# MLP second product: the fifth sub-product beside the sixth, the seventh and the fourth alone, and one weight combination made by transfers

## Chip, cores and metric

One core of a Trainium2 chip runs the whole program. The metric is device time in microseconds (us), the median of repeated executions; times in the profile come from one further execution that the hardware profiler recorded. Engines are named as in the profile: PE (matrix multiply), PEld (its weight loads), DVE (vector), ACT (activation), POOL, SP. SP, ACT and POOL also issue transfers (DMA).

## The reference

One layer of a diffusion backbone, fp32. Only its last third matters here, the MLP with its normalised and gated residual:

```python
def _sq_relu_mlp(h, w1, w2):
    return jnp.square(jax.nn.relu(h @ w1)) @ w2
...
        y_x = _sq_relu_mlp(_modulate(x, g_pre_mlp[l], sh2, sc2), w_mlp_in[l], w_mlp_out[l])
        x = x + gt2 * _rmsnorm(y_x, g_post_mlp[l])
```

`x` is 1024 tokens by 1024, the hidden layer 4096 wide. The second product, hidden (1024x4096) by `w2` (4096x1024), is the subject.

## The kernel before

**Products.** Each fp32 matmul is made of three on numbers split into a high part (`..h`, rounded, by ACT, line 169) and a low part (`..l`, the rest, by DVE, line 175): high·high, low·high, high·low (`three`, lines 221 to 223). The second product is one level of a seven-product scheme (Strassen-Winograd). With A the 2x2 blocks of the hidden layer (rows: token halves; columns: interleaved halves of the 4096) and B those of `w2`, it needs

- P1 = A11·B11, P2 = A12·B21, P4 = A22·T4, P5 = S1·T1, P6 = S2·T2, P7 = S3·T3, and a third one, S4·B22, which is itself made of seven smaller products (`INNER`, M1 to M7);
- of the weights T1 = B12−B11, T2 = B22−T1, T3 = B22−B12, T4 = T2−B21 (one sign is kept the other way round in the code);
- results: C11 = P1+P2; u2 = P1+P6; u4 = u2+P5; C12 = u4 + third; C22 = u4+P7; C21 = u2+P7 with P4.

C11 and C12 are the two halves of the output of tokens 0 to 511 (rows 0 to 3, 128 tokens each), C21 and C22 those of tokens 512 to 1023 (rows 4 to 7).

**Stages.** A product runs over 8 groups g of the 4096 (`NG`), and in each over four token tiles t: 24 matmuls of 128x512 (`group`). Its sums stand in four PSUM banks: `pyx` (P1, P2), `pyy` (P6), `pyv` (P7, then P4 on top of it), `pyz` (P5). The order of the groups is the list `items`; at the start of each group `prepare()` makes the operands of an item three places ahead: load the hidden block (`hr..`), load and combine weights, split both. The profile leaves out the first digit of a name: `t_4h` is `t1_4h` to `t4_4h`; `hrS`, `hhS` are of S1, S2, S3, `hrA`, `hhA` of A11, A12, A22; `b` are blocks of `w2`.

Before the change the order is P6 with P7 by turns (8 groups each), then P4 groups 0 to 3 by turns with P5 groups 0 to 3, then P5 groups 4 to 7, then P4 groups 4 to 7, the last two stretches token tile by token tile at the end, so that a tile can be finished when its sums end. In P6, DVE makes T1, T3 and T2 from loads of B12 and B22 (lines 2053 to 2056); for P4 it loads B22 and B21 again and makes T4 from them (lines 2063, 2064).

**Finishing a row.** `gated`: ACT squares and sums a half row (line 154), DVE multiplies it by the gate (line 2200); `finish` also asks for the inverse root of both halves' sums (DVE line 161, POOL line 163, `ry`); `end` multiplies the row by it, adds the residual (`xo`, loaded from `x1d`; DVE line 2208) and sends it out (line 2209). Row 7 is done in quarters at the very end (`pyw` is a second bank for its second quarter; lines 2217, 2348, 2352, 2354, 2357).

**Order and buffers.** In this part PE, ACT, DVE and SP keep the order in which the code is written; POOL keeps its own program order. Loads of weights use 4 buffers (`wraw`), hidden loads 4 (`tmp` "h"), weight splits 4 pairs (`whl`), all else a pool of 33 pages (`page`). An instruction that needs a buffer waits until its last user is done.

Of the kernel before, what the change touches and what calls it, by code (L numbers as in the profile page):

```python
# [18 lines left out]
P = 128  # L19
# [3 lines left out]
NT = SEQ // P  # L23
# [80 lines left out]
def hybrid_block(ctx, tc, x, ctx_in, w_mod, mod_pages, w_u, b_mod, gp1, gp2, w_in, pool_w, rpb, w_out, w1, w2, vectors,  # L104
# [1414 lines left out]
    with tc.tile_pool(name="ps2", bufs=6, space=PSUM) as ps2:  # L1519
# [7 lines left out]
      with ExitStack() as tmp2:  # L1527
# [487 lines left out]


        w2v = w2.rearrange("(k i p) n -> i p k n", i=2, p=P)
        t1, t3 = {}, {}
# [5 lines left out]
        def wcols(name, i, h, g):  # L2024
            return columns(wraw.tile([P, 1024], F32, tag="raw", name=f"{name}_{g}"), i, h, g)
# [15 lines left out]
        def operands(name, g, made=None):  # L2041
            made = made or high_low
            if name == "P1":
                t1[g] = columns(page(f"b11_{g}"), 0, 0, g)
                return hidden("A11", g, g <= AHEAD + 1), made(f"b11_{g}", t1[g])
            if name == "P2":
                return hidden("A12", g), made(f"b21_{g}", wcols("b21", 1, 0, g))
            if name in INNER:
                return inner_operands(name, g)
            if name == "P6":  # L2050

                b12, b22 = wcols("b12", 0, 1, g), wcols("b22", 1, 1, g)
# [10 lines left out]
            nc.vector.tensor_tensor(b22, b22, t1[g], sub)  # L2063
            nc.vector.tensor_tensor(b21, b21, b22, sub)
# [96 lines left out]
        with tc.issue_after(first[ET.PE]), in_order(ET.PE, ET.Activation, ET.DVE, ET.SP):  # L2161
# [5 lines left out]
            def four(name):  # L2167
                return [bank(f"{name}_{t}") for t in range(4)]
# [37 lines left out]
            def end():  # L2206
                for m, rs, xt in ending:
                    nc.vector.scalar_tensor_tensor(xt, rows[m], rs, xt, mul, add)  # L2208
# [83 lines left out]
            for t in range(4):  # L2292
                rows[t] = page(f"row{t}")
                gated(t, 0, x[t])
            y, v = four("pyy"), four("pyv")
            for g in range(NG):
                group(y, "P6", g)
                if g == NG - 1:
                    u2 = halves("u2")
                    for t in range(4):  # L2300
                        nc.vector.tensor_tensor(u2[t], y[t], s1[t], add)
                group(v, "P7", g)
            for t in range(4):
                rows[4 + t] = page(f"row{4 + t}")
                nc.vector.tensor_tensor(half(4 + t, 1), v[t], u2[t], add)
            z = four("pyz")
            u4 = [inner_part(f"c{t // 2}")[:, t % 2 * 512 : t % 2 * 512 + 512] for t in range(4)]
            for g in range(NG // 2):
                group(v, "P4", g, more=True, last=(g == NG // 2 - 1))
                group(z, "P5", g)  # L2310
                nc.vector.tensor_tensor(u4[g], u4[g], u2[g], add)
            for g in range(NG // 2, NG - 2):
                group(z, "P5", g)
            while coming:
                prepare()

            for t in range(4):
                cs = slice(0, 512 if t < 3 else 256)
                nc.vector.tensor_tensor(v[t][:, cs], v[t][:, cs], u2[t][:, cs], add)
            xts = {}  # L2320
            for m in range(4):
                xts[m] = wraw.tile([P, 1024], F32, tag="raw", name=f"xo{m}")
            for m in range(4, NT):
                xts[m] = page(f"xo{m}")
            for m in range(NT):
                nc.sync.dma_start(xts[m], x1d[m])
# [64 lines left out]
```

## Time and profile before

| | us |
|---|---|
| median of 3 runs | 1027.67 (1027.49 to 1028.32) |
| the profiled execution, its own time | 1027.31 |
| its span, first to last instruction | 1025.5 |
| what lies around the span | 1.8 |
| PE busy | 1006.3 (98% of the span) |
| DVE busy | 795.2 (78%) |
| ACT busy | 559.4 (55%) |
| POOL busy | 154.6 (15%) |

"Busy" of PE is modelled, since matmuls overlap. A timeline row reads: start, duration, engine, line, operation, output<-inputs, shape, and in brackets the engine's idle time before it with what released it. In the part in question, P6 starts at 836.6 us and the last matmul at 1014.0 us.

### The profile page before, as it was taken

What the parts mean: (1) busy time and instruction counts of PE and PEld (TensorE: products, weight loads), DVE (VectorE), ACT (ScalarE), POOL (GpSimd) and SP (SyncE); (2) the same over time, 40 slices, a digit from 0 to 9 for tenths busy, and PEclk for the clock granted to TensorE, in tenths of its full rate; (3) what the DMA queues carried; (4) which work ended last, traced back from release to release, by engine and by line L of the source; (5) the groups of instructions that cost most, each with busy time, mean ns of one, the idle gap of its engine ahead of it and who ended that gap; (6) DMA issues with size and microseconds to landing.
All of it is one profiled execution on the core that took longest, in us unless ns stands there. A gap on an engine that the chain in (4) does not pass through costs nothing. (4 is left out here: it accounts for less than half of the span.)

```text
span 1025.5 us, 16659 instructions
## 1 busy us (share of the span) xinstructions
PE 1006.3 (98%) x6154; PEld 838.3 (82%) x6154; DVE 795.2 (78%) x1217; ACT 559.4 (55%) x974; POOL 154.6 (15%) x234
## 2 busy tenths in 40 slices
PE   8999999999999999999999999999999999999995
PEld 5788888878998888888888888888888888887874
DVE  5588757977885788879988888656787898768587
ACT  6672354348886747786554554546564444334333
POOL 4111200266773221400000000000000000000001
PEclk9999999999999999999999999999999999999998
DMA  9899898541447946886876567348976766554374
GB/s 363 316 294 302 262 262 286 205 103 43 104 98 204 235 169 200 278 216 208 265 255 216 184 210 257 123 159 268 335 267 213 263 246 229 197 194 173 114 285 166
DMA packets 126594, 224.85 MB, mean 219 GB/s; under 512 B 9584, under 2 KB 61680, under 8 KB 126512
## 3 DMA queue, kind: packets, MB, share of 16 engines
q1 hardware_dynamic: 100016, 173.24, 49.9%
q0 software_dynamic: 9360, 19.58, 9.3%
q10 hardware_dynamic: 17136, 30.97, 8.1%
q8 instruction: 48, 0.79, 0.3%
q14 instruction: 34, 0.28, 0.1%
HBM read 170.25 MB, written 52.45 MB: 217 GB/s over the span
## 5 line engine op out<-in xcount | busy, mean ns | idle before, releaser
L1234 ACT ACTIVATE sp<-sp,nm 128x640 f32<-128x640 f32 (+1 forms) x64 | 51.3, 802 | 10.9 <-DVE ri L1238 5.1
L1223 DVE CUSTOM_DVE_ANT_0 sp<-S,tab 128x640 f32<-128x640 f32 (+1 forms) x56 | 44.5, 795 | 14.0 <-PE pz L1254 9.1
L1857 ACT ACTIVATE c<-c 128x512 f32<-128x512 f32 x48 | 30.3, 632 | 44.3 <-DVE c L1979 25.0
L169 ACT CAST wpS<-S 128x512 fp32r<-128x512 f32 x64 | 38.7, 616 | 28.0 <-PE phv L223 10.1
L221 PE MATMUL phx<-thB,wpA 128*128 128x512 f32 x128 | 50.2, 392 | 0.0
L223 PE MATMUL phx<-thB,wpA 128*128 128x512 f32 x128 | 49.8, 389 | 0.0
L222 PE MATMUL phx<-tlB,wpA 128*128 128x512 f32 x128 | 49.8, 389 | 0.0
L175 DVE TENSOR_TENSOR wpS<-S,wpS 128x512 fp32r<-128x512 f32 x64 | 43.4, 686 | 7.5 <-ACT wpS L169 7.5
L163 POOL TENSOR_TENSOR ry<-vy,nhalf 128x1 f32<-128x1 f32 x7 | 5.4, 767 | 285.0 <-DVE vy L161 285.0
L1858 ACT ACTIVATE c<-c 128x512 f32<-128x512 f32 x48 | 30.3, 631 | 15.1 <-DVE sa L1942 12.1
L221 PEld LDWEIGHTS phx<-thB,wpA 128*128 128x128 f32 x128 | 24.0, 188 | 5.5 <-ACT s L1910 0.4
L223 PEld LDWEIGHTS phx<-thB,wpA 128*128 128x128 f32 x128 | 24.0, 188 | 5.1
L222 PEld LDWEIGHTS phx<-tlB,wpA 128*128 128x128 f32 x128 | 24.0, 188 | 4.9
L1273 DVE COPY pt<-T 128x512 f32<-128x512 f32 x32 | 21.9, 686 | 5.6 <-PE T L1254 5.6
L1288 PE MATMUL pa<-pt,v 128*64 128x128 f32 x352 | 25.9, 279 | 0.2
L221 PE MATMUL phz<-thB,wpS 128*128 128x512 f32 x64 | 25.0, 391 | 0.0
L221 PE MATMUL phv<-thT,wpA 128*128 128x512 f32 x64 | 25.0, 391 | 0.0
L223 PE MATMUL phv<-thT,wpA 128*128 128x512 f32 x64 | 24.9, 389 | 0.0
L223 PE MATMUL phz<-thB,wpS 128*128 128x512 f32 x64 | 24.9, 389 | 0.0
L222 PE MATMUL phz<-tlB,wpS 128*128 128x512 f32 x64 | 24.9, 389 | 0.0
L222 PE MATMUL phv<-tlT,wpA 128*128 128x512 f32 x64 | 24.9, 389 | 0.0
L221 PE MATMUL phy<-thT,wpS 128*128 128x512 f32 x64 | 24.9, 389 | 0.0
(1178 smaller groups left out, 3553.6 us busy)
## 6 DMA issues: line engine op xcount, KB each, us to landing
b<-in_w SPq DMA_DIRECT2D x48, 512.0 KB, 4.3
hrA<-hdA SPq DMA_DIRECT2D x24, 512.0 KB, 5.5
hrS<-hdS SPq DMA_DIRECT2D x24, 512.0 KB, 5.3
wm<-in_mod_pages SPq DMA_DIRECT2D x16, 512.0 KB, 9.4
wa_0w<-in_w SPq DMA_DIRECT2D x16, 512.0 KB, 5.0
wa_1w<-in_w SPq DMA_DIRECT2D x16, 512.0 KB, 4.3
hdA<-c ACTq DMA_DIRECT2D x32, 256.0 KB, 2.2
hdS<-sa ACTq DMA_DIRECT2D x32, 256.0 KB, 2.2
```

The costliest lines, as they stand in the source:

```text
L163: nc.gpsimd.tensor_tensor(r, v, nhalf, ALU.pow)
L169: nc.scalar.copy(hi, src)
L175: nc.vector.tensor_tensor(lo, src, hi.bitcast(F32), sub)
L221: nc.tensor.matmul(ps, ahi, bhi, start=first, stop=False, skip_group_check=more)
L222: nc.tensor.matmul(ps, ahi, blo, start=False, stop=False, skip_group_check=more)
L223: nc.tensor.matmul(ps, alo, bhi, start=False, stop=last, skip_group_check=more)
L1223: nc.vector.tensor_tensor_reduce(out=to, in0=s, in1=bt, scale=1.0, scalar=BIG, op0=add, op1=ALU.min, accum_out=nm)
L1234: nc.scalar.activation(sp, sp, AF.Exp, bias=least[i, e], scale=-1.0, accum_out=sums[i][:, e : e + 1])
L1273: copy(turns[i].rearrange("p e i t -> p (e i) t")[:, :, h * HD : (h + 1) * HD], turned[i][h].rearrange("p (a t) -> p a t", a=8))
L1288: nc.tensor.matmul(pa[e * HD : (e + 1) * HD, cols], v[:, f : f + HD], turns[i][:, e, c] if c < 4 else fifths[i][:, :, (e + 1) * HD : (e + ...
L1857: nc.scalar.activation(r, src, AF.Relu)
L1858: nc.scalar.activation(r, r, AF.Square)
```

## The change

P5 takes the place of P7 beside P6; then come the 8 groups of P7, then the 8 of P4, of which the last four are done token tile by token tile as before.

- T3 is still made beside T1 and T2, but P7 comes later now: POOL stores it to DRAM (`t3d`), and SP loads it again for P7 (8 stores, 8 loads of 512 KB).
- T2 goes to a page of its own, with its sign turned (its split turns it back, line 177 instead of 175). After the split, a transfer issued by POOL adds B21 from DRAM to that page (`last_added`, `add_to`), which makes T4: 8 adding transfers of 512 KB. The second loads of B22 and B21 (16 of 512 KB) and DVE's lines 2063 and 2064 (8 each) go.
- u4 is made from `pyz` and u2 when P5 is complete, C12 from it; rows 0 to 3 are finished while P7 runs, one per group from the second on, and sent out by POOL. The residuals of rows 0 to 3 are loaded in P7's first four groups, those of rows 4 to 7 at the end.
- C22 is made after P7; its squares and gate products stand in P4's first four groups.

```diff
-                nc.vector.tensor_tensor(b12, b22, b12, sub)
-                t3[g] = b12
-                nc.vector.tensor_tensor(b22, b22, t1[g], sub)
-                return hidden("S2", g), made(f"t2_{g}", b22)
+                t2[g] = page(f"t2_{g}")
+                nc.vector.tensor_tensor(t2[g], t1[g], b22, sub)
+                nc.vector.tensor_tensor(b12, b22, b12, sub)
+                nc.gpsimd.dma_start(t3d[g], b12)
+                parts = hidden("S2", g), high_low(f"t2_{g}", t2[g], -1.0)
+                if g < NG - 2:
+                    last_added(g)
+                return parts
...
             if name == "P7":
-                return hidden("S3", g), made(f"t3_{g}", t3.pop(g))
-            b22, b21 = wcols("b22", 1, 1, g), wcols("b21", 1, 0, g)
-            nc.vector.tensor_tensor(b22, b22, t1[g], sub)
-            nc.vector.tensor_tensor(b21, b21, b22, sub)
-            return hidden("A22", g), made(f"t4_{g}", b21)
+                r = wraw.tile([P, 1024], F32, tag="raw", name=f"t3_{g}")
+                nc.sync.dma_start(r, t3d[g])
+                if g in (2, 3):
+                    last_added(NG - 4 + g)
+                return hidden("S3", g), made(f"t3_{g}", r)
+            return hidden("A22", g), made(f"t4_{g}", t2.pop(g))
+        t3d = [dram.tile([P, 1024], F32, tag=f"t3_{g}", name=f"t3_{g}") for g in range(NG)]
+        def last_added(g):
+            add_to(t2[g].rearrange("p (a f) -> p a f", a=2), w2v[1][:, 2 * g : 2 * g + 2, :512])
...
-        items += [(n, g) for g in range(NG) for n in ("P6", "P7")]
-        items += [(n, g) for g in range(NG // 2) for n in ("P4", "P5")] + [("P5", g) for g in range(NG // 2, NG)]
-        items += [("P4", g) for g in range(NG // 2, NG)]
+        items += [(n, g) for g in range(NG) for n in ("P6", "P5")]
+        items += [(n, g) for n in ("P7", "P4") for g in range(NG)]
...
-                    nc.sync.dma_start(og[m], xt)
+                    (nc.gpsimd if m < 4 else nc.sync).dma_start(og[m], xt)
...
-            y, v = four("pyy"), four("pyv")
+            y, z = four("pyy"), four("pyz")
...
+                group(z, "P5", g)
+            def residual(m):
+                xts[m] = page(f"xo{m}")
+                nc.sync.dma_start(xts[m], x1d[m])
+            v, u4 = four("pyv"), halves("u4")
+            for g in range(NG):
                 group(v, "P7", g)
+                if g < 4:
+                    residual(g)
+                    nc.vector.tensor_tensor(u4[g], z[g], u2[g], add)
+                    nc.vector.tensor_tensor(c12[g], c12[g], u4[g], add)
+                if 0 < g < 5:
+                    finish(g - 1, 1, c12[g - 1], xts[g - 1])
+            end()
             for t in range(4):
                 rows[4 + t] = page(f"row{4 + t}")
-                nc.vector.tensor_tensor(half(4 + t, 1), v[t], u2[t], add)
+                nc.vector.tensor_tensor(half(4 + t, 1), v[t], u4[t], add)
             for g in range(NG // 2):
                 group(v, "P4", g, more=True, last=(g == NG // 2 - 1))
-                group(z, "P5", g)
-                nc.vector.tensor_tensor(u4[g], u4[g], u2[g], add)
-            for g in range(NG // 2, NG - 2):
-                group(z, "P5", g)
-            while coming:
-                prepare()
+                gated(4 + g, 1, half(4 + g, 1))
+            side = bank("pyw")[:, :256]
             for t in range(4):
                 cs = slice(0, 512 if t < 3 else 256)
                 nc.vector.tensor_tensor(v[t][:, cs], v[t][:, cs], u2[t][:, cs], add)
-            for t in range(4):
-                token_sums(z, t, [made["P5", g] for g in (NG - 2, NG - 1)], False, True, False)
-                c = half(4 + t, 1)
-                nc.vector.tensor_tensor(c, c, z[t], add)
-                gated(4 + t, 1, c)
-                finish(t, 1, z[t], xts[t], u4[t])
-                if t == 1:
-                    side = bank("pyw")[:, :256]
-                    nc.vector.tensor_tensor(side, v[3][:, 256:], u2[3][:, 256:], add)
+            nc.vector.tensor_tensor(side, v[3][:, 256:], u2[3][:, 256:], add)
+            while coming:
+                prepare()
+            for m in range(4, NT):
+                residual(m)
```

Three places in the order of instructions, before and after. First DVE where P7 ends and P4's first group is to go on top of its sums; `u2` is u2, `row4` to `row7` take C22. Before:

```order
L2301 TENSOR_TENSOR u21_9816<-pyy_3_9252,s11_8547 128x512
L2063 TENSOR_TENSOR b22_1_9821<-b22_1_9821,b11_1_8043 128x1024
L2064 TENSOR_TENSOR b21_1_9823<-b21_1_9823,b22_1_9821 128x1024
L175 TENSOR_TENSOR hhA22_1l_9830<-hrA22_1_9827,hhA22_1h_9829 128x1024
L175 TENSOR_TENSOR t4_1l_9834<-b21_1_9823,t4_1h_9833 128x1024
L2305 TENSOR_TENSOR row4_9861<-pyv_0_9253,u20_9815 128x512
L2305 TENSOR_TENSOR row5_9863<-pyv_1_9254,u20_9815 128x512
```

After:

```order
L175 TENSOR_TENSOR hhA22_2l_10194<-hrA22_2_10191,hhA22_2h_10193 128x1024
L175 TENSOR_TENSOR t4_2l_10198<-t2_2_9310,t4_2h_10197 128x1024
L2217 SCALAR_TENSOR_TENSOR xo3_10065<-row3_9259,ry_3_10120,xo3_10065 128x1024
L2332 TENSOR_TENSOR row4_10227<-pyv_0_9886,u40_9890 128x512
L2332 TENSOR_TENSOR row5_10229<-pyv_1_9887,u40_9890 128x512
```

The sum for u2 and the two steps that make a T4 no longer stand ahead of the copies of P7's sums; the last step of row 3 does.

Second, DVE where P4's last four groups begin (`pyv` gets u2 added there) and what follows. Before:

```order
L2063 TENSOR_TENSOR b22_7_10267<-b22_7_10267,b11_7_8400 128x1024
L2064 TENSOR_TENSOR b21_7_10269<-b21_7_10269,b22_7_10267 128x1024
L175 TENSOR_TENSOR hhA22_7l_10276<-hrA22_7_10273,hhA22_7h_10275 128x1024
L175 TENSOR_TENSOR t4_7l_10280<-b21_7_10269,t4_7h_10279 128x1024
L2319 TENSOR_TENSOR pyv_0_9253<-pyv_0_9253,u20_9815 128x512
L2319 TENSOR_TENSOR pyv_1_9254<-pyv_1_9254,u20_9815 128x512
L2319 TENSOR_TENSOR pyv_2_9255<-pyv_2_9255,u21_9816 128x512
L2319 TENSOR_TENSOR pyv_3_9256<-pyv_3_9256,u21_9816 128x256
L2330 TENSOR_TENSOR row4_9861<-row4_9861,pyz_0_9869 128x512
L2200 TENSOR_TENSOR row4_9861<-row4_9861,Gb_8997 128x512
L2222 TENSOR_TENSOR c0_10319<-pyz_0_9869,c0i_8916 128x512
```

After:

```order
L2339 TENSOR_TENSOR pyv_0_9886<-pyv_0_9886,u20_9843 128x512
L2339 TENSOR_TENSOR pyv_1_9887<-pyv_1_9887,u20_9843 128x512
L2339 TENSOR_TENSOR pyv_2_9888<-pyv_2_9888,u21_9844 128x512
L2339 TENSOR_TENSOR pyv_3_9889<-pyv_3_9889,u21_9844 128x256
L2340 TENSOR_TENSOR pyw_10383<-pyv_3_9889,u21_9844 128x256
L175 TENSOR_TENSOR hhA22_7l_10392<-hrA22_7_10389,hhA22_7h_10391 128x1024
L175 TENSOR_TENSOR t4_7l_10396<-t2_7_9699,t4_7h_10395 128x1024
L161 SCALAR_TENSOR_TENSOR vy_4_10435<-sy0_8087,sy1_8088 128x1
L2209 TENSOR_TENSOR row4_10227<-pyv_0_9886,Gb_9005 128x512
L2217 SCALAR_TENSOR_TENSOR xo4_10399<-row4_10227,ry_4_10437,xo4_10399 128x1024
```

Between the additions to `pyv` and row 4's last half there is now one operand split instead of the second halves of rows 4 to 7 and all of rows 0 to 3; that split stood ahead of the additions before.

Third, POOL's queue, after the gate of the MLP was set up (`gb`). Before, only the seven inverse roots follow:

```order
L276 DMA gb_8204<-accb_7162 16x1x16 x4
L163 TENSOR_TENSOR ry_0_10325<-vy_0_10323,nhalf_79 128x1
L163 TENSOR_TENSOR ry_1_10352<-vy_1_10350,nhalf_79 128x1
L163 TENSOR_TENSOR ry_2_10381<-vy_2_10379,nhalf_79 128x1
L163 TENSOR_TENSOR ry_3_10408<-vy_3_10406,nhalf_79 128x1
```

After, the first of the transfers:

```order
L276 DMA gb_8212<-accb_7170 16x1x16 x4
L2057 DMA t3_0_5131<-b12_0_9123 128x1024
L211 DMA t2_0_9128<-in_w2 128x2x512
L2057 DMA t3_1_5132<-b12_1_9203 128x1024
L211 DMA t2_1_9208<-in_w2 128x2x512
```

Eight such pairs come first now, then the inverse roots, the stores of rows 0 to 3 between the first four.

More of the change, by code (lines that the diff above doesn't have):

```diff
@@ L2017, in hybrid_block @@
         w2v = w2.rearrange("(k i p) n -> i p k n", i=2, p=P)
-        t1, t3 = {}, {}
+        t1, t2 = {}, {}
         def columns(raw, i, h, g):
@@ L2301, in hybrid_block @@
                         nc.vector.tensor_tensor(u2[t], y[t], s1[t], add)
-                group(v, "P7", g)
+                group(z, "P5", g)
+            xts = {}
+            def residual(m):
+                xts[m] = page(f"xo{m}")
+                nc.sync.dma_start(xts[m], x1d[m])
+            v, u4 = four("pyv"), halves("u4")
+            c12 = [inner_part(f"c{t // 2}")[:, t % 2 * 512 : t % 2 * 512 + 512] for t in range(4)]
+            for g in range(NG):
+                group(v, "P7", g)
+                if g < 4:
[5 more added lines that the diff above has]
+            end()
             for t in range(4):
                 rows[4 + t] = page(f"row{4 + t}")
-                nc.vector.tensor_tensor(half(4 + t, 1), v[t], u2[t], add)
-            z = four("pyz")
-            u4 = [inner_part(f"c{t // 2}")[:, t % 2 * 512 : t % 2 * 512 + 512] for t in range(4)]
+                nc.vector.tensor_tensor(half(4 + t, 1), v[t], u4[t], add)
             for g in range(NG // 2):
                 group(v, "P4", g, more=True, last=(g == NG // 2 - 1))
-                group(z, "P5", g)
-                nc.vector.tensor_tensor(u4[g], u4[g], u2[g], add)
-            for g in range(NG // 2, NG - 2):
-                group(z, "P5", g)
-            while coming:
-                prepare()
+                gated(4 + g, 1, half(4 + g, 1))
+            side = bank("pyw")[:, :256]
             for t in range(4):
@@ L2319, in hybrid_block @@
                 nc.vector.tensor_tensor(v[t][:, cs], v[t][:, cs], u2[t][:, cs], add)
-            xts = {}
-            for m in range(4):
-                xts[m] = wraw.tile([P, 1024], F32, tag="raw", name=f"xo{m}")
+            nc.vector.tensor_tensor(side, v[3][:, 256:], u2[3][:, 256:], add)
+            while coming:
+                prepare()
             for m in range(4, NT):
-                xts[m] = page(f"xo{m}")
-            for m in range(NT):
-                nc.sync.dma_start(xts[m], x1d[m])
-            for t in range(4):
-                token_sums(z, t, [made["P5", g] for g in (NG - 2, NG - 1)], False, True, False)
-                c = half(4 + t, 1)
-                nc.vector.tensor_tensor(c, c, z[t], add)
-                gated(4 + t, 1, c)
-                finish(t, 1, z[t], xts[t], u4[t])
-                if t == 1:
-                    side = bank("pyw")[:, :256]
-                    nc.vector.tensor_tensor(side, v[3][:, 256:], u2[3][:, 256:], add)
+                residual(m)
             late = [made["P4", g] for g in range(NG // 2, NG)]
```

## The prediction

> **What bounds the kernel now.** First the page's head and its table of engines, to see which engine fills the span.
>
> ```profile
> span 1025.5 us, 16659 instructions
> PE 1006.3 (98%) x6154; PEld 838.3 (82%) x6154; DVE 795.2 (78%) x1217; ACT 559.4 (55%) x974; POOL 154.6 (15%) x234
> ```
>
> PE is the bound, and the change leaves its matmuls as they are. Time can only come from places where PE stands still and from what follows its last matmul. So second the busy times by stretch, over the second product: P6 with P7, then P4 and P5, then the last four P4 groups, then the tail.
>
> ```profile
> 836.00:924.00 88.00, 88.00 (x388) 72.29 (x386) 71.40 (x65) 36.26 (x43) 0.00 (x0) 1.00 0.57 197
> 924.00:992.00 68.00, 65.65 (x290) 54.10 (x289) 50.46 (x49) 25.09 (x25) 0.00 (x0) 1.00 0.49 174
> 992.00:1014.00 22.00, 22.00 (x119) 19.15 (x120) 17.42 (x30) 9.11 (x25) 4.08 (x5) 1.00 0.50 193
> 1014.00:1022.00 8.00, 0.28 (x3) 0.08 (x1) 7.50 (x15) 1.04 (x5) 1.29 (x3) 0.81 0.65 262
> ```
>
> Columns: stretch, length, busy PE, PEld, DVE, ACT, POOL, PE clock, DMA share, GB/s. PE is full in the first and third, misses 2.35 us in the second and is done in the fourth, where DVE works 7.50 of 8 us: the tail is DVE's. 388 matmuls in 88 us are 0.227 us each, so a group of 24 takes 5.44 us.
>
> Third PE's timeline around the two gaps of the second stretch.
>
> ```profile
> 923.63 0.39 PE L223 MATMUL pyv<-t_7h,hhS_7l 128*128 128x512 f32 x1
> 924.84 0.47 PE L221 MATMUL pyv<-t_0h,hhA_0h 128*128 128x512 f32 x1 [0.82 <-DVE row L2305]
> ...
> 990.01 0.39 PE L223 MATMUL pyz<-t_7h,hhS_7l 128*128 128x512 f32 x1
> 991.93 0.47 PE L221 MATMUL pyv<-t_4h,hhA_4h 128*128 128x512 f32 x1 [1.53 <-DVE pyv L2319]
> ```
>
> Matmuls start 0.23 apart when nothing waits; here the starts are 1.21 and 1.92 apart, so 0.98 and 1.69 us are lost, 2.67 together. DVE is late both times: with the copies of P7's sums (line 2305), and with adding u2 to them (line 2319).
>
> Fourth the tail, from the last matmul on.
>
> ```profile
> 1014.00 0.28 PE L223 MATMUL pyw<-t_7h,hhA_7l 128*128 128x256 f32 x1
> ...
> 1014.38 0.38 ACT L154 ACTIVATE jy<-pyw 128x256 f32<-128x256 f32 x1
> 1014.66 0.19 ACT L154 ACTIVATION_READ_ACCUMULATOR jy<-pyw 128x1 f32 x1
> 1020.17 0.29 ACT L2352 ACTIVATE root_y<-whole_y,rest_y 128x1 f32<-128x1 f32 x1 [5.32 <-DVE rest_y L2348]
> ...
> 1014.23 1.28 DVE L2208 SCALAR_TENSOR_TENSOR xo<-row,ry,xo 128x1024 f32<-128x1024 f32 x1
> ...
> 1018.39 1.28 DVE L2208 SCALAR_TENSOR_TENSOR xo<-row,ry,xo 128x1024 f32<-128x1024 f32 x1
> 1019.60 0.42 DVE L2217 TENSOR_TENSOR row<-pyv,Gb 128x256 f32<-128x256 f32 x1
> 1019.93 0.15 DVE L2348 SCALAR_TENSOR_TENSOR rest_y<-sy,sy 128x1 f32<-128x1 f32 x1
> 1020.00 0.42 DVE L2217 TENSOR_TENSOR row<-pyw,Gb 128x256 f32<-128x256 f32 x1
> 1020.50 0.16 DVE L2354 RECIPROCAL inverse_y<-root_y 128x1 f32<-128x1 f32 x1
> 1020.70 1.54 DVE L2357 SCALAR_TENSOR_TENSOR xo<-row,inverse_y,xo 128x512 f32<-128x512 f32 x3
> ```
>
> ACT has row 7's last squares at 1014.85, but its root waits 5.32 us for DVE, which still finishes rows 4 to 6 because rows 0 to 3 came first.
>
> **The change part by part.**
>
> *The tail.* In the last stretch (three tiles of 5.44 us, then two quarters) DVE will have, for each of rows 4 to 6, one sum (0.15), one gate product and one row step, beside one operand split at its start. The prices:
>
> ```profile
> L2063 DVE TENSOR_TENSOR b<-b,b x8: 1216/1218/1219, 904.3 to 986.3; 128x1024 f32<-128x1024 f32 x8
> L2064 DVE TENSOR_TENSOR b<-b,b x8: 1224/1225/1226, 905.6 to 987.6; 128x1024 f32<-128x1024 f32 x8
> L2208 DVE SCALAR_TENSOR_TENSOR xo<-row,ry,xo 128x1024 f32<-128x1024 f32 x7 | 9.0, 1280 | 0.8 <-POOL ry L163 0.4
> L2200 DVE TENSOR_TENSOR row<-pyv,Gb 128x512 f32<-128x512 f32 x3 | 2.1, 684 | 0.0
> 988.86 1.06 ACT L169 CAST t_7h<-b 128x1024 fp32r<-128x1024 f32 x1 [1.15 <-DVE b L2064]
> ```
>
> That is 0.15+0.68+1.28 = 2.1 us in each 5.44: no backlog. With E the end of the last matmul (1014.28 now), the chain is: ACT's squares done at E+0.57 (1014.85 now), root 0.29 to E+0.90, reciprocal from E+0.94, the last row step 0.20 later at E+1.14 (1020.50 to 1020.70 now), and from there to the end of the span the 4.80 us of now (1020.70 to 1025.5). Row 7's product from `pyw` (0.42, from E+0.6) fits beside the root. The span ends at E+5.94; now it is E+11.22. Gain 5.28.
>
> *Gap at P7's end.* In P7's last group, counted from its start, ACT splits `t4_2` as its buffer comes free (to 1.1), DVE takes the low part (1.22, to 2.35), row 3's last step (1.28, to 3.6) and row 4's copy (0.68, to 4.3; tile 0's sums are there at 1.4). PE wants it at 5.44. The gap of 0.98 goes.
>
> *Gap before the last stretch.* The sums of tile 0 are complete 4.08 us before P4's fourth group ends, and DVE's earlier work there is only operand splits that wait for nothing recent. The gap of 1.69 goes. Late next is group 7's split, which now stands behind the additions: after the group's end 0.42+0.42 for `pyv` and `pyw`, 2x1.22 for the split, about 0.2 of starting, 3.5 us; PE uses it after 18 matmuls, 4.1 us. It passes with 0.6 to spare; were it 1 us late, PE would lose 0.4.
>
> *P7 with rows 0 to 3 beside it.* Per group two splits (2.44); in the first four two sums (1.36); four times each of sum, product and row step (2.1). Over eight groups 8x2.44+4x1.36+4x2.1 = 33.4 of 43.5 us; groups 2 and 3 take 5.9 of 5.44, absorbed by operands made three groups ahead.
>
> *P6 with P5.* DVE's work per pair stays three combinations and four splits (8.6 of 10.9 us); one split becomes line 177's form, 0.06 dearer by 1280 against 1220 ns, hidden. Lines 2063 and 2064 go: 16 operations, 19.5 us of DVE; where PE was not waiting for them that is worth nothing.
>
> *Transfers.* Out go 16 loads, in come 8 loads, 8 stores, 8 adding ones. Their new place is P6 with P5: beside four loads per pair one store and one adding transfer. B22's next load now waits for the store (its buffer is B12's old one), and SP's queue behind it: hidden loads of the same group, all wanted some 20 us later. Prices of POOL's transfers, and what a stretch full of adding ones took (433 to 450 us, 17 us):
>
> ```profile
> x<-xr POOLq DMA_DIRECT2D x8, 512.0 KB, 5.0
> to_2w<-in_w_out POOLq DMA_DIRECT2D x1, 512.0 KB, 9.4
> to_3w<-in_w_out POOLq DMA_DIRECT2D x1, 512.0 KB, 11.3
> b<-in_w SPq DMA_DIRECT2D x48, 512.0 KB, 4.3
> q0 software_dynamic: 576, 2.10, 69.3%
> q10 hardware_dynamic: 17136, 30.97, 8.1%
> ```
>
> Adding: 0.693x17/2.10 = 5.6 us of all sixteen engines per MB, 2.9 for 0.52 MB. The store: 2.7 per MB by the plain stores (8.1% of 1025.5 over 30.97), 1.4, or 2.9 at the adding price. The loads: 0.57x10.9 = 6.2. Sum 10.5 to 12.0 of 10.9 us, so the engines are just full, at worst 1.1 us over per pair, 9 us over eight. What covers that is DVE's lead:
>
> ```profile
> 865.67 1.23 DVE L175 TENSOR_TENSOR t_4l<-b,t_4h 128x1024 fp32r<-128x1024 f32 x1
> 880.33 0.39 PE L221 MATMUL pyy<-t_4h,hhS_4h 128*128 128x512 f32 x1
> ```
>
> P6's operand of group 4 is ready 13.4 us before PE takes it. 9 is under 13.4: I take nothing, and keep 0 to 3 us for the range.
>
> The Trainium skill ("DMA: Bandwidth & Descriptors", Anatomy of one DMA, SWDGE path) fits POOL's transfers with 2.0 us plus bytes over 436 GB/s, an estimate of 3.2 us for one of these; by it a pair's store and adding would fill the engines for 2.4 us, 8.6 of 10.9 in all, and rival C below had no chance. The rows' 5.0 to 11.3 us to landing disagree, and the rows decide.
>
> *Sum.* −5.28−0.98−1.69 = −7.95 against the profiled execution's own 1027.31 (span 1025.5 and 1.81 around it): 1019.4. The median is 0.36 above that execution: **1019.7**.
>
> **The rivals.**
>
> *A: PE's stops remain or move* (the late split, a residual or T3 load late in P7). For it: the spare of 0.6 us, and four loads or stores per group in P7's first half. Against: the sums above. The tail is won all the same: 1027.7−5.3 = 1022.4, or 1020.5 with one stop of 1 us.
>
> *B: DVE stays behind in the last stretch*, because rows 0 to 3 or the squares of C22 slip. Against: 33.4 of 43.5 us. Only the gaps are won: 1025.0.
>
> *C: slower, the adding transfers fill the transfer engines.* P6 and P5 run at their pace. For it: 10.5 to 12.0 of 10.9 us. If adding beside loads cost twice its price (5.8), a pair would take 6.2+2.9+5.8 = 14.9, 32 us over in eight, less the 13.4 lead 18.6: 1038. It decides from a pair of 13.6 us on (8x2.7−13.4 = 8). Against: that needs 7.4 for store and adding, where the rows give 4.3 to 5.8.
>
> *D: POOL's issuing and DVE's operations keep each other out.* An issue on POOL took 0.86 to 2.08 us:
>
> ```profile
> L211 POOL DMA_DIRECT2D to_3w<-in_w_out x1: 2079/2079/2079, 341.2 to 341.2; - x1
> 346.72 0.86 POOL L211 DMA_DIRECT2D to_3w<-to_3w  x1 [1.94 <-DMA to_3w<-to_1w]
> L175 DVE TENSOR_TENSOR to_0l<-to_2w,to_0h x3: 1219/1224/1227, 347.0 to 381.1; 128x1024 fp32r<-128x1024 f32 x3
> ```
>
> If DVE stood still for 2.08 us twice per pair, it would need 8.6+4.2 = 12.8 of 10.9, 15 us over in eight, 1.8 beyond the lead: 1021.5. Against: DVE's split begins at 347.0, inside POOL's issue from 346.72 to 347.58, and takes its usual 1.22. The Trainium skill ("SBUF — State Buffer", Who interferes with whom) says that a VectorE instruction with two SBUF inputs and a GpSimd one that reads SBUF exclude each other; that issue and that split do not show it.
>
> **How the numbers follow.** Forecast 0.74; A 0.13; B 0.04; C 0.07; D 0.02. 0.2% (2.1 us) is about what a measurement of this kernel tells from no change. Faster by more: forecast, A, D and most of B, 0.92; within: 0.02; slower: C's part above 1029.8, 0.06. Range: low 1018.6 (last stores landing sooner, and run to run 0.05%); high 1023.0, A's end and 0.6 for the transfers; outside lie B and C, 0.11.
>
> **What would show it.** PE without a stop over 0.3 us between 842 and its end; that end at 1011.6; root 0.1 us behind ACT's last squares; DVE's row steps of rows 0 to 3 between P7's groups 2 and 7. Wrong: PE waiting for `t_..l` or `hhS` in P6 and P5 with the DMA share near 1 (C); PE's gap at the last stretch on `t_7l` (A); `rest_y` or a row step ending the root's wait (B).

## The result, and the profile after

The changed kernel takes **1018.33 us** (median of 5 runs, 1018.14 to 1018.68), the kernel before, on the same chip, 1027.53 (1027.45 to 1028.32): a ratio of 0.9909, 95% interval 0.9895 to 0.9924. That is 9.2 us less. The forecast was 1019.7 with a range from 1018.6: direction and mechanism came, the time lies 0.3 us under the range.

The page of the changed kernel, head and engines:

```profile
span 1016.9 us, 16662 instructions
...
PE 1006.8 (99%) x6154; PEld 838.8 (82%) x6154; DVE 771.6 (76%) x1197; ACT 558.8 (55%) x974; POOL 173.5 (17%) x254
```

PE's work is the same (1006.8 against 1006.3 us), the span is 8.6 us shorter: all of it came from where PE had stood still. The four stretches of the prediction, in the same columns:

```profile
836.00:924.00 88.00, 87.83 (x388) 72.41 (x387) 66.63 (x62) 36.25 (x43) 12.45 (x14) 1.00 0.96 304
924.00:992.00 68.00, 68.00 (x302) 56.31 (x301) 49.33 (x58) 29.47 (x41) 7.22 (x8) 1.00 0.49 171
992.00:1014.00 22.00, 19.14 (x108) 16.63 (x106) 8.92 (x17) 4.79 (x13) 1.66 (x3) 1.00 0.19 75
1014.00:1022.00 8.00, 0.00 (x0) 0.00 (x0) 0.00 (x0) 0.00 (x0) 0.00 (x0) 0.71 0.17 60
```

The second stretch is now full (65.65 before), so both gaps are gone. In the third DVE works 8.92 us (17.42 before), and in the fourth, where it had worked 7.50, nothing is left. The first stretch's DMA share went from 0.57 to 0.96.

The timeline of the changed kernel: the only stop of PE from P6's start on (0.17 us), the last steps of rows 0 and 3 inside P7, and the tail.

```profile
839.17 0.50 PE L221 MATMUL pyy<-t_0h,hhS_0h 128*128 128x512 f32 x1 [0.17 <-DVE row L2209]
...
938.03 1.28 DVE L2217 SCALAR_TENSOR_TENSOR xo<-row,ry,xo 128x1024 f32<-128x1024 f32 x1
963.91 1.28 DVE L2217 SCALAR_TENSOR_TENSOR xo<-row,ry,xo 128x1024 f32<-128x1024 f32 x1
...
1010.86 0.28 PE L223 MATMUL pyw<-t_7h,hhA_7l 128*128 128x256 f32 x1
1011.74 0.29 ACT L2361 ACTIVATE root_y<-whole_y,rest_y 128x1 f32<-128x1 f32 x1
1011.74 0.42 DVE L2226 TENSOR_TENSOR row<-pyw,Gb 128x256 f32<-128x256 f32 x1 [2.40 <-ACT jy L154]
...
1012.27 1.54 DVE L2366 SCALAR_TENSOR_TENSOR xo<-row,inverse_y,xo 128x512 f32<-128x512 f32 x3
```

The last matmul ends at 1011.14, and from there to the end of the span it is 5.76 us (11.22 before). Where ACT's root waited 5.32 us for DVE, now DVE waits 2.40 us for ACT.

### The profile page after: what moved, and what is told of

It is laid out like the page before. It is cut to its first block, busy times and chain, and to the rows that moved or that the text cites. A ratio compares the mean times of both kernels' runs of the same rounds, so it can differ in the third digit from the quotient of the medians.

```text
span 1016.9 us, 16662 instructions
## 1 busy us (share of the span) xinstructions
PE 1006.8 (99%) x6154; PEld 838.8 (82%) x6154; DVE 771.6 (76%) x1197; ACT 558.8 (55%) x974; POOL 173.5 (17%) x254
## 4 chain that ended last, share of the span: by engine, by line
PE 92%; ACT 3%; DVE 2%; DMA 2%; issue 1%; SPq 0%; ACTq 0%; POOL 0%; DVEq 0%
PE pu L476 4%; PE pa L1288 4%; PE S L1208 3%; PE phz L221 3%; PE phv L221 3%; PE pyv L222 3%; PE phv L222 3%; PE pyv L221 3%; PE phz L222 3%; PE pyv L223 3%; PE phz L223 3%; PE phv L223 3%; PE pyx L221 3%; PE pyx L222 3%; PE pyx L223 3%; PE phx L221 2%
## 5 line engine op out<-in xcount | busy, mean ns | idle before, releaser
L1234 ACT ACTIVATE sp<-sp,nm 128x640 f32<-128x640 f32 (+1 forms) x64 | 51.3, 802 | 10.5 <-DVE ri L1238 5.1
L1858 ACT ACTIVATE c<-c 128x512 f32<-128x512 f32 x48 | 30.3, 631 | 15.9 <-DVE sa L1942 12.1
L2057 POOL DMA_DIRECT2D t<-b x8 | 4.6, 573 | 145.1 <-DVE b L2056 145.1
```

What stands on the lines that cost most here:

```text
L1234: nc.scalar.activation(sp, sp, AF.Exp, bias=least[i, e], scale=-1.0, accum_out=sums[i][:, e : e + 1])
L1858: nc.scalar.activation(r, r, AF.Square)
```

## Experiments: the order, the relief of DVE, or both

The change has two parts that both take work from DVE's list ahead of the end: the order (rows 0 to 3 finished in P7) and T4 made by transfers. First each was tried alone. The first two kernels of this section, the two of the next section and the kernel before ran on one chip (before: 1026.73); the third one ran on another.

**The new order, T4 on DVE as before.**

```diff
+            b22, b21 = wcols("b22", 1, 1, g), wcols("b21", 1, 0, g)
+            nc.vector.tensor_tensor(b22, b22, t1[g], sub)
+            nc.vector.tensor_tensor(b21, b21, b22, sub)
-            return hidden("A22", g), made(f"t4_{g}", t2.pop(g))
+            return hidden("A22", g), made(f"t4_{g}", b21)
...
```

> The new order with the old way of making T4: B22 and B21 are loaded again in front of P4 and DVE makes T4 from them; no adding transfers. Theory (the order brings the gain, and the place freed on DVE is what lets the order work): DVE has 2.44 us more per P4 operand, 4.9 + 0.6 of 5.44 us per group beside the copies of C22 (2.7). PE loses about 1 us at P7's end, 2 to 3 us before the last four groups and up to 2 us at group 7's split: 1020 to 1024, 1022.5 likeliest. Rival 1 (only the order matters, DVE has room): 1018.0 to 1018.7 and no stop of PE over 0.3 us. Rival 2 (only the relief of DVE matters): 1026 to 1028.

Measured: 1023.37 (1022.89 to 1023.81), ratio 0.9966 (0.9954 to 0.9979), 3.4 us less than before. The timeline of PE:

```profile
991.54 0.47 PE L221 MATMUL pyv<-t_4h,hhA_4h 128*128 128x512 f32 x1 [2.02 <-DVE pyv L2336]
996.90 0.50 PE L221 MATMUL pyv<-t_7h,hhA_7h 128*128 128x512 f32 x1 [1.03 <-ACT t_7h L169]
998.16 0.51 PE L222 MATMUL pyv<-t_7l,hhA_7h 128*128 128x512 f32 x1 [0.76 <-DVE t_7l L175]
```

The two stops expected in the last stretch came (2.02, and 1.79 at group 7's split); the one at P7's end did not. Without the transfers the new order buys its short tail with these 3.8 us of stops.

**The old order, T4 by transfers.**

```diff
-                nc.vector.tensor_tensor(b22, b22, t1[g], sub)
-                return hidden("S2", g), made(f"t2_{g}", b22)
+                t2[g] = page(f"t2_{g}")
+                nc.vector.tensor_tensor(t2[g], t1[g], b22, sub)
+                parts = hidden("S2", g), high_low(f"t2_{g}", t2[g], -1.0)
+                add_to(t2[g].rearrange("p (a f) -> p a f", a=2), w2v[1][:, 2 * g : 2 * g + 2, :512])
+                return parts
...
```

> The order of before, with T4 made by adding transfers (the second loads of B22 and B21 and their two DVE steps go; T3 stays in its load buffer). Theory (the order is what counts): DVE's additions before the last stretch come about 1.1 us earlier and the stop at P7's end (0.98) goes, the late list stays: about 1025.4 (1024 to 1026.5). Rival (the relief of DVE by 19.5 us is what counts): 1018.5 to 1021.

Measured: 1020.74 (1020.63 to 1020.92), ratio 0.9941 (0.9928 to 0.9955): 6.0 us less, so the theory that the order is what counts fell, and the rival was right. DVE over the stretch that leads up to the additions before, and over the same stretch in this kernel:

```profile
969.50:991.00 21.50, 20.90 (x93) 16.98 (x91) 19.92 (x17) 8.22 (x9) 0.00 (x0) 1.00 0.61 213
```

```profile
969.50:991.00 21.50, 21.50 (x96) 17.82 (x95) 13.76 (x18) 8.29 (x11) 0.91 (x1) 1.00 0.48 165
```

Before, DVE was busy 19.92 of 21.50 us here, mostly with the last four operands of P4, each with T4's two steps. Those steps hid behind PE, but not behind DVE's own later list. When that list begins and ends, before:

```profile
991.09 2.22 DVE L2319 TENSOR_TENSOR pyv<-pyv,u 128x512 f32<-128x512 f32 x4
1020.00 0.42 DVE L2217 TENSOR_TENSOR row<-pyw,Gb 128x256 f32<-128x256 f32 x1
```

and with T4 by transfers:

```profile
984.16 2.22 DVE L2319 TENSOR_TENSOR pyv<-pyv,u 128x512 f32<-128x512 f32 x4
1013.31 0.42 DVE L2217 TENSOR_TENSOR row<-pyw,Gb 128x256 f32<-128x256 f32 x1
```

The list starts 6.93 us earlier and ends 6.69 earlier. P6 itself began 0.66 earlier in this profile (835.92 against 836.58), so 6.3 and 6.0 us are the kernel's.

**The old order without T4's steps, its loads kept.** This tells DVE's time from the loads.

```diff
-            nc.vector.tensor_tensor(b22, b22, t1[g], sub)
-            nc.vector.tensor_tensor(b21, b21, b22, sub)
```

> The kernel before without its two DVE steps per T4 (T4 is then B21 as loaded; B22 is still loaded, and nobody reads it). Theory (DVE's 2.44 us per operand, one for one in the late list, since DVE was busy 20.5 of the 21.5 us before it): 1020.7 as with T4 by transfers (1020 to 1021.5). Rival (the 16 loads and their buffers held things up): 1024 to 1027.

Measured: 1021.00 (1020.97 to 1021.98) beside 1026.74, ratio 0.9944 (0.9932 to 0.9956). Its timeline:

```profile
984.38 2.22 DVE L2317 TENSOR_TENSOR pyv<-pyv,u 128x512 f32<-128x512 f32 x4
```

The list begins within 0.22 us of the kernel with transfers: it is DVE's time, not the loads. Whether the two gains add can't be told from these runs: 3.4 and 6.0 alone make 9.4, both together gave 9.2 in the first measurement and 8.6 when it was repeated (1018.01 against 1026.65, below), and each gain is known to about 1.3 us.

## Experiments: what finishing rows 0 to 3 early is worth

**Rows 0 to 3 after the additions.** (`finish` and the sum to C12 leave P7.)

```diff
-                    nc.vector.tensor_tensor(c12[g], c12[g], u4[g], add)
-                if 0 < g < 5:
-                    finish(g - 1, 1, c12[g - 1], xts[g - 1])
...
+            for t in range(4):
+                nc.vector.tensor_tensor(c12[t], c12[t], u4[t], add)
+                finish(t, 1, c12[t], xts[t])
             late = [made["P4", g] for g in range(NG // 2, NG)]
```

> The changed kernel, but rows 0 to 3 are finished (sum to C12, gate product, row step) only after the additions that open the last stretch; C22's squares and gate products stay in P4's first four groups. Theory (the tail is a matter of DVE's backlog against its idle time): the four rows are 4 x 2.66 = 10.6 us of DVE; DVE now idles 12.5 us between 992.2 and row 7's last product at 1011.74, so the end moves by 0 to 1 us: 1018.3 to 1019.3. Rival (each row finished late costs its time at the end, as in the kernel before, where the tail was 5.28 us longer): 1022 to 1024.

Measured: 1018.78 (1018.69 to 1018.96), ratio 0.9922 (0.9910 to 0.9934). Row 7's last product in its timeline stands where the changed kernel has it:

```profile
1011.74 0.42 DVE L2226 TENSOR_TENSOR row<-pyw,Gb 128x256 f32<-128x256 f32 x1
```

Against its last matmul, which ends at 1010.62, that is 0.5 us later than in the changed kernel: 10.6 us more of DVE's work in the last stretch went into the 12.5 us that it idles there in the changed kernel, and cost half a microsecond.

**All finishing late, as before.** (C12's and C22's sums with P5, squares, products and rows 0 to 3 all after the additions.)

```diff
+            for t in range(4):
+                c = half(4 + t, 1)
+                nc.vector.tensor_tensor(c, c, z[t], add)
+                gated(4 + t, 1, c)
+                finish(t, 1, z[t], xts[t], c12[t])
...
```

> The changed kernel, but the whole finishing is put back to where the kernel before has it: after the additions, for each of four tiles, P5's sums are added to C22's half and to C12, both are squared and gated, and the row of C12 is finished. P7's place, T4 by transfers and the early split stay. Theory (DVE's late list decides the end, PE's two stops are a separate matter): the list starts at 992.2 instead of 993.22 and then takes as long as before (row 7's last product at 1020.00 before), so that product comes at about 1019.0 instead of 1011.74: 1025.5 (1024.0 to 1026.5), PE without its two stops. Rival (the two stops of PE and the tail add up one by one): the tail alone, 1018.3 + 5.3 = 1023.6. Rival (the finishing was not the matter): 1018 to 1019.

Measured: 1025.95 (1025.88 to 1027.20), ratio 0.9993 (0.9985 to 1.0002). Its last matmul, the start of DVE's list and row 7's last product:

```profile
1010.87 0.28 PE L223 MATMUL pyw<-t_7h,hhA_7l 128*128 128x256 f32 x1
...
991.72 0.68 DVE L2340 TENSOR_TENSOR row<-row,pyz 128x512 f32<-128x512 f32 x1
...
1019.54 0.42 DVE L2226 TENSOR_TENSOR row<-pyw,Gb 128x256 f32<-128x256 f32 x1
```

PE ends where the changed kernel's does, without a stop, and the program is hardly faster than before: with the list as long as that, the 2.67 us of PE's gaps are worth nothing. The product came at 1019.54, expected at 1019.0. T4 comes by transfers here as in the old order that won 6.0 us, where the list began at 984.16; here it begins at 991.72, because in the new order the additions ahead of it wait for P4's first four groups, which now come right before. So the new order needs part of the finishing early; that rows 0 to 3 alone may be late, the run before shows.

## Experiments: how near the transfers are to costing time

**More transfers in P6 and P5, not held in place.** One adding transfer of 512 KB per pair into an unread page, then two into two pages, then one plain load.

```diff
                     last_added(g)
...
+                for s in spare:
+                    add_to(s.rearrange("p (a f) -> p a f", a=2), w2v[1][:, 2 * g : 2 * g + 2, :512])
                 return parts
```

> The changed kernel with one more adding transfer of 512 KB per pair of P6 and P5, into a page that nobody reads. Theory (the transfer engines are full: 0.96 of the 88 us, at 1.03 to 1.05 between 836 and 902; an adding transfer costs 2.9 us of all sixteen): a pair then needs 10.44 + 2.9 = 13.3 of 10.9 us, 2.4 over, 19.5 over eight pairs, less the 13.9 us by which P6's operands lie ahead: plus 6, 1024 (1020 to 1030), PE waiting in P6's last groups on hrS, b or their splits. Rival (the busy shares hold waiting, and an adding transfer costs little more than its bytes, 1.2 us): 11.6 of 10.9, 6 over eight, covered: 1018.3 to 1018.8.

> As the one before with two more adding transfers per pair, into two pages that nobody reads. Theory: 16.2 of 10.9 us per pair, 43 over eight less 13.9: plus 29, 1047 (1038 to 1052). Rival: 12.8 of 10.9, 15 over eight, 1 beyond the lead: 1019 to 1021.

> The changed kernel with one more plain load of the same 512 KB per pair, by the same queue into a page that nobody reads. Theory (a plain transfer costs 1.4 us of all sixteen): 11.8 of 10.9, 7.5 over eight, covered by the 13.9 us of lead: 1018.3 to 1018.9, no stop of PE. Rival (the engines are full, and each further byte is lost at once): plus 7, 1025.

Measured, beside 1026.65: 1032.85 (1030.98 to 1034.33; ratio 1.0059, 1.0047 to 1.0071), 1042.17 (1041.93 to 1042.44), and 1022.34 (1020.44 to 1025.96). All lost time against the changed kernel (1018.01, below), the plain load too. But these kernels were not what they were meant to be. The extra transfers depend on nothing but each other, and in the order of the first kernel they stand earlier on POOL's queue, two to a pair in the first four pairs:

```
L211 DMA spare0_9143<-in_w2 128x2x512
L211 DMA t2_1_9211<-in_w2 128x2x512
L211 DMA spare0_9143<-in_w2 128x2x512
L211 DMA spare0_9143<-in_w2 128x2x512
L2057 DMA t3_2_5133<-b12_2_9309 128x1024
```

The timeline of that kernel shows what follows. T3 of group 2 was made by 846.10, and its store went out at 863.83, behind extra transfers that waited for one another; the next load of a weight block waited for the store to land, DVE 12.38 us for the load, and in the end PE for DVE. The lead took up most of this first wait; one pair later DVE waited another 9.85 us in the same way, and PE stopped for 6.36.

```profile
844.88 1.22 DVE L2056 TENSOR_TENSOR b<-b,b 128x1024 f32<-128x1024 f32 x1
...
863.11 1.20 POOL L211 DMA_DIRECT2D spare<-in_w  x1 [8.13 <-DMA b<-in_w]
863.83 1.06 POOL L2057 DMA_DIRECT2D t<-b  x1
...
876.67 1.23 DVE L2055 TENSOR_TENSOR t<-b,b 128x1024 f32<-128x1024 f32 x1 [12.38 <-DMA b<-in_w]
...
901.64 0.79 PE L221 MATMUL pyy<-t_5h,hhS_5h 128*128 128x512 f32 x1 [6.36 <-ACT t_5h L171]
```

**The same load issued by ACT; the line of T3's store moved behind that of the pair's adding transfer; T3 in a page of its own, alone and with the extra transfers.**

```diff
...
+                nc.scalar.dma_start(s.rearrange("p (a f) -> p a f", a=2), w2v[1][:, 2 * g : 2 * g + 2, :512])
```
```diff
-                nc.gpsimd.dma_start(t3d[g], b12)
                 parts = hidden("S2", g), high_low(f"t2_{g}", t2[g], -1.0)
                 if g < NG - 2:
                     last_added(g)
+                nc.gpsimd.dma_start(t3d[g], b12)
```
```diff
-                nc.vector.tensor_tensor(b12, b22, b12, sub)
-                nc.gpsimd.dma_start(t3d[g], b12)
+                t3 = page(f"t3p_{g}")
+                nc.vector.tensor_tensor(t3, b22, b12, sub)
+                nc.gpsimd.dma_start(t3d[g], t3)
```

> The changed kernel with one more plain load of 512 KB per pair as in the run with such a load on POOL's queue (1022.34), but issued by ACT, into two pages in turn that nobody reads, so that POOL's queue stays as it is. Theory (POOL's queue and the chain through the store, not the bytes): 1018.0 to 1019.5, no stop of PE over 0.5 us. Rival (the bytes: the transfer engines are full): 1022 again, 1020 to 1025.

> The changed kernel with one line moved: T3's store stands on POOL's queue behind the adding transfer of the same pair, no byte more. Theory (what the extra transfers broke is a chain: T3's store on POOL, its buffer free, SP's next load of B22 into it, the next T3; where nothing paces it, two pairs of it take 17.4 us, 847.00 to 864.46, against 21.8 at PE's pace, so 4.4 us of slack): the store comes 2.9 us later, inside the slack: 1018.0 to 1018.6. Rival (no slack is left): plus 3 to 10.

> The changed kernel with T3 made into a page of its own and stored from there, nothing added. Theory: PE has no stop to win back, so 1018.0 to 1018.6, with the first loads of P6 and P5 landing earlier against PE. Rival (the freer chain crowds the loads and something else comes late): 1019 to 1021.

> The kernel with one more adding transfer per pair (1032.85), with T3 made into a page of its own and stored from there, so that the load buffer is free as soon as DVE has made T3 and no load waits for a store. Theory (chain): most of the 14.8 us goes, 1018.5 to 1022. Rival (full transfer engines): 1030 to 1034 again.

Measured, beside 1026.81: 1018.18 (1017.72 to 1018.36) with ACT's load, 1017.94 (1017.50 to 1018.52) with the line moved, 1018.34 (1017.67 to 1018.94) with T3's page: none differs from the changed kernel. So the plain load's bytes cost nothing. The moved line tests nothing: POOL's queue of that kernel, which keeps an order of its own, still has the store first and the adding transfer 2.27 us behind it, as the changed kernel has (847.00 and 849.27).

```profile
846.33 0.57 POOL L2060 DMA_DIRECT2D t<-b  x1 [6.99 <-DVE b L2056]
848.60 1.21 POOL L211 DMA_DIRECT2D t<-in_w  x1 [1.70 <-DVE t_2l L177]
```

It is the changed kernel once more, and how much slack the chain through the store has is not shown by it. The fourth took 1034.23 (1033.45 to 1034.74), a miss for the theory: freeing the load buffer alone did not help. DVE stood there 15.16 us before the split of S1's group 3, with no releaser named. T3's page stays taken until its store, still behind the extra transfers, has landed; that another buffer waits for that page is argued, not shown.

**Extra transfers that keep their place.** A one-column write by DVE ahead of each, and two pages in turn for each, so that none waits for another.

```diff
...
+                for s in spare[g % 2 :: 2]:
+                    nc.vector.memset(s[:, :1], 0.0)
+                    add_to(s.rearrange("p (a f) -> p a f", a=2), w2v[1][:, 2 * g : 2 * g + 2, :512])
```

> The changed kernel with one more adding transfer per pair, into two unread pages in turn; a one-column DVE write ahead of each keeps it in its pair, and it waits for no other transfer. Theory (what cost 14.8 us was the wait of one adding transfer for another on POOL's queue, with T3's stores behind it): 1018.0 to 1020. Rival (adding transfers at 2.9 us of the full engines): plus 6 to 13, 1024 to 1031.

> The same with one more plain load per pair on POOL's queue, paced as the adding ones (unpaced it took 1022.34). Theory (queue): 1018.0 to 1018.8, as the load by ACT. Rival (POOL's transfers are dearer than ACT's): 1021 to 1024.

> The same with two more adding transfers per pair, into four unread pages. Theory (queue): the engines still have to move 11.5 MB more by some 16 us per pair at the price of 2.9 against 10.9, so here the bytes should show: 1025 to 1045. Rival (a busy share of 1 is no limit at all): 1018 to 1021.

Measured, beside 1026.74: one adding transfer 1018.02 (1017.72 to 1018.12), one plain load 1018.42 (1018.17 to 1018.80), two adding ones 1036.98 (1036.77 to 1037.96; ratio 1.0100, 1.0084 to 1.0115). So the 14.8 us were the queue, and the kernel has room for one more adding transfer but not for two. Not all that the two cost is theirs: their four pages have to be filled first, DVE waited 3.49 us for that up to 831.55, and PE then stopped for 2.76 us in P6's first group. The operands of P6 tell the pace from there on, in the views of the tiles; the start of the split is the number before "to". The changed kernel, then one more, then two more:

```profile
L177 DVE SCALAR_TENSOR_TENSOR t_4l<-t,t_4h x1: 1216/1216/1216, 865.2 to 865.2; 128x1024 fp32r<-128x1024 f32 x1
L177 DVE SCALAR_TENSOR_TENSOR t_7l<-t,t_7h x1: 1217/1217/1217, 897.9 to 897.9; 128x1024 fp32r<-128x1024 f32 x1
L222 PE MATMUL pyy<-t_7l,hhS_7h x8: 389/389/389, 913.0 to 917.7; 128*128 128x512 f32 x8
```

```profile
L177 DVE SCALAR_TENSOR_TENSOR t_4l<-t,t_4h x1: 1220/1220/1220, 869.4 to 869.4; 128x1024 fp32r<-128x1024 f32 x1
L177 DVE SCALAR_TENSOR_TENSOR t_7l<-t,t_7h x1: 1217/1217/1217, 905.6 to 905.6; 128x1024 fp32r<-128x1024 f32 x1
L222 PE MATMUL pyy<-t_7l,hhS_7h x8: 389/389/389, 912.4 to 917.2; 128*128 128x512 f32 x8
```

```profile
L177 DVE SCALAR_TENSOR_TENSOR t_4l<-t,t_4h x1: 1220/1220/1220, 875.4 to 875.4; 128x1024 fp32r<-128x1024 f32 x1
L177 DVE SCALAR_TENSOR_TENSOR t_7l<-t,t_7h x1: 1217/1217/1217, 919.5 to 919.5; 128x1024 fp32r<-128x1024 f32 x1
```

Three pairs take 32.7 us in the changed kernel (10.9 each: PE sets the pace), 36.2 with one more (12.1), 44.1 with two (14.7). If the transfers set the pace in the last two kernels, the step from 12.1 to 14.7 gives 2.6 us per adding transfer, and 12.1−2.6 = 9.5 us for a pair of the change as it is; both are estimates. Where PE does not yet hold it back, the changed kernel took 8.7 us per pair (two from 847.00 to 864.46, by T3's stores). What DVE waits for in both kernels is the load behind T3's store (3.1 to 4.1 us at a time with two more), and the store lands later with each adding transfer on its queue: in 7.7, 8.6 and 16.9 us. So 2.6 may be the growth of this chain as well as a price of the engines; no run tells them apart. With one more, the operand of group 7 is ready at 906.8 and used at 912.4: the lead still lasts, at 5.6 us; in the changed kernel it is 13.9 (899.1 to 913.0).

**The changed kernel again.**

> The changed kernel again, nothing edited, on the chip of the next three. Theory (the 0.45 us by which the part before line 2015's products ran shorter in the changed kernel's profile is a difference from one execution to the next): the start of P6 falls anywhere between 835.9 and 836.7 us, where it lay in the five other profiles, and the time is 1018.3 with 0.5 either way. Rival (the change shortens the earlier part too): P6 starts within 0.1 us of 836.1 again.

Measured: 1018.01 (1017.66 to 1018.23) beside 1026.65, ratio 0.9914 (0.9902 to 0.9927). P6's first matmul in the timelines of the kernel before, of the changed kernel, and of the changed kernel again:

```profile
836.58 0.39 PE L221 MATMUL pyy<-t_0h,hhS_0h 128*128 128x512 f32 x1
```
```profile
836.12 0.39 PE L221 MATMUL pyy<-t_0h,hhS_0h 128*128 128x512 f32 x1
```
```profile
835.61 0.39 PE L221 MATMUL pyy<-t_0h,hhS_0h 128*128 128x512 f32 x1
```

Eighteen profiles, with the same matmuls ahead of P6, put it between 835.6 and 837.3; both orders lie on both sides of 836.5. The earlier part is not shortened by the change; it differs between executions by more than a microsecond.

## Why the prediction was right in its mechanism, and where it failed

- **The tail.** Forecast: the span ends 5.94 us after the last matmul; measured 5.76, a gain of 5.46 for 5.28. The chain (last squares, root, reciprocal, row steps) came as written. The reason given, that rows 0 to 3 came first in DVE's list, was only a part: with those rows late again half a microsecond was lost, with all finishing late 7.6 to 7.9, and with T4's steps gone the old order won 6.0 us. The tail is DVE's whole list against its idle time.
- **T4's steps "worth nothing" where PE does not wait.** Half wrong: they also delayed DVE's own list by 6.3 us, as the two kernels without them show (6.1 in the second). In the sum this did not show, since the tail had been credited in full to the early rows.
- **Both gaps of PE**, 2.67 us: gone, as forecast. The late split of group 7 had 0.6 us to spare by the forecast; `t_7l` was done at 992.26 and used at 993.2, 0.94.
- **P7 with rows 0 to 3 beside it**: 33.4 of 43.5 us of DVE forecast, 32.01 in the trace. Line 177's form of the split cost 1.22 us like the other, not 1.28.
- **Transfers at no cost**: right, and the lead did not shrink at all. Mis-sized: 10.5 to 12.0 us per pair forecast, against 8.7 for the pairs that PE does not hold back and 9.5 by the estimate above; 2.9 for an adding transfer, 2.6 by that estimate.
- **The rivals.** A and B did not occur. C lay further off than its 10.5 to 12.0 us said: a lead of 13.9 us over eight pairs allows 10.9+13.9/8 = 12.6 per pair, between the 12.1 with one adding transfer more and the 14.7 with two. A second way to C was not on the list: transfers that wait for each other on POOL's queue, with T3's stores behind. D did not occur; in the timeline DVE's split and POOL's issue overlap for 0.84 us, and both take what they usually do, 1.22 and 1.20 us:

```profile
877.23 1.22 DVE L175 TENSOR_TENSOR hhS_5l<-hrS,hhS_5h 128x1024 fp32r<-128x1024 f32 x1
...
877.61 1.20 POOL L211 DMA_DIRECT2D t<-in_w  x1 [1.69 <-DVE t_5l L177]
```

 The Trainium skill's rule ("SBUF — State Buffer", Who interferes with whom), weighed in the forecast, is not seen here either.
- **The step that failed is the last one of the sum, the level:** 0.36 added for the median, and 0.05% allowed from run to run. The profiled executions differ by 1027.31−1018.63 = 8.68 us, 0.73 more than the −7.95 of the sum: 0.46 because P6 began earlier, 0.18 in the tail, 0.08 around the span. Another 0.66 came from putting the median 0.36 above the profiled execution, where it now lies 0.30 below. Together 1.4. The low end, 1018.6, had allowed 0.05% from run to run; the start of P6 alone differs by three times that between profiles. The medians say the same: beside the experiments, on four chips, the kernel before took 1026.65 to 1026.81, not the 1027.67 that the sum started from, and the changed kernel took 1018.01 on one of them. Of the 8.64 us between the two there, the gaps (2.67) and the tail (5.46) make 8.13 by the first two traces; what the last 0.5 is stays open.

The forecast set the transfers' landing against the Trainium skill's formula ("DMA: Bandwidth & Descriptors", Anatomy of one DMA, SWDGE path), by an estimate 3.2 us for one of 512 KB. The changed kernel's issues in P6 and P5 disagree again:

```profile
t<-b POOLq DMA_DIRECT2D x7, 512.0 KB, 7.7
t<-in_w POOLq DMA_DIRECT2D x7, 512.0 KB, 8.9
```

## What to carry to other kernels

Work that hides behind the bounding engine is not free if its own engine has a list that ends last: count that engine's list up to the end against its idle time, and expect little from shortening it further once idle time is left (half a microsecond for 10.6 us here). Try the parts of a change one by one: here the relief of DVE, which the forecast had held to be worth nothing outside PE's waits, won 6.0 us alone, and the order, credited with the whole tail, 3.4. Do not put an absolute time to better than the executions agree: here about 1.5 us.

## What the hardware showed that was not expected

**A DMA share of 1 was not the limit.** The changed kernel moved 304 GB/s at a share of 0.96. With one more plain load per pair, by ACT and then by POOL, the windows read:

```profile
836.00:924.00 88.00, 88.00 (x390) 72.83 (x389) 66.85 (x61) 36.33 (x42) 12.44 (x14) 1.00 1.03 348
```
```profile
836.00:924.00 88.00, 88.00 (x389) 72.77 (x389) 67.48 (x69) 36.48 (x43) 17.69 (x21) 1.00 1.02 352
```

44 to 48 GB/s more for 0.06 to 0.07 of share, and no time lost. A share above 1 can't be busy time alone; that packets under way beside each other are counted more than once is argued, not shown. The pace of the operands told the limit better.

**After a stop of some microseconds PE runs at half its clock.** In the first kernel with extra transfers, around the stop of 6.36 us that ended at 901.64 (column PE clock, third from the end):

```profile
899.00:901.60 2.60, 0.00 (x0) 0.00 (x0) 1.28 (x2) 2.00 (x2) 0.59 (x1) 0.72 1.07 295
901.60:904.00 2.40, 1.71 (x3) 1.11 (x4) 2.13 (x3) 1.79 (x2) 0.68 (x1) 0.50 1.05 341
```

A matmul took 0.79 us there for 0.39, and the clock was back at 1.00 from 908 on. Of that kernel's 14.8 us the four stops make 9.5; the clock of 0.88 and 0.89 in the two stretches of 22 us around them makes, by an estimate, another 5. The length of a single stop does not decide. With T4 on DVE a stop of 2.02 us left the clock at 1.00, and so did the 1.03 and 0.76 us with little work between them. In the kernel above, 1.53 and 0.95 us (before 883) were followed by 0.52; with two more adding transfers, 2.38 us (before 919.36) and 2.76 us were followed by 0.50:

```profile
841.63 0.50 PE L221 MATMUL pyy<-t_0h,hhS_0h 128*128 128x512 f32 x1 [2.76 <-DVE row L2216]
843.00:845.00 2.00, 2.00 (x6) 1.55 (x5) 2.00 (x3) 0.11 (x1) 1.91 (x2) 0.50 1.04 353
```

The Trainium skill ("TensorE: Matmul & The Clock Gate", Part 1: The HAM clock gate) says that the clock falls to half after an idle window of about 3.4 us and needs as long a busy one to return. The 0.50 after 6.36 us agrees, and so do the 4.0 us until the matmuls started 0.23 us apart again after the stop that ended at 841.63; that 2.38 us and 2.76 us were enough does not, and here the runs decide.
